# Exchanging softmax statistics between two key sets on VectorE instead of through DRAM

## The chip, the cores and the metric

The kernel runs on one core of a Trainium2 chip. The core has TensorE (PE, matrix products into PSUM), VectorE (DVE), ScalarE (ACT), GpSimd (POOL), and SyncE (SP), which here only issues DMAs. The metric is the device time in microseconds. A separate execution carries the profiler; the trace, the page and every row quoted come from that one. TensorE's clock can be throttled, and the profile lists the granted share of full speed.

## The reference

One block of a hybrid model on 1024 tokens of width 1024, all in fp32. What matters here is the attention part:

```python
q = rms_norm(q.reshape(B, S, N_HEADS, HEAD_DIM), q_norm_g[l]) * HEAD_DIM ** -0.5
k = rms_norm(k.reshape(B, S, N_HEADS, HEAD_DIM), k_norm_g[l])
for window, dilation in ((128, 1), (512, 4), (2048, 16)):
    o_g, lse_g = dilated_window_attention(q, k, v, slopes, window, dilation)
    outs.append(o_g); lses.append(lse_g)
mix = jax.nn.softmax(jnp.stack(lses), axis=0)
o = jnp.einsum('gbsh,gbshd->bshd', mix, jnp.stack(outs))
y_b = o @ w_attn_out[l]
```

There are 16 heads of 64 columns, with a linear distance penalty per head. Each query sees three sets of keys: the last 128 tokens, every fourth token of the last 512, every sixteenth of the last 2048. The three softmaxes, mixed by their log sums, are one softmax in which a key counts as often as it occurs. Beside attention there are a gated convolution branch, gates (a sigmoid of a product of the normed input), an output product and a feed-forward block with a short convolution.

## The kernel before

**Stages.** First come the normed input and a part of the gate and convolution products; then six column groups of queries, keys and values (`qkv_head`, `qkv_tail`, lines 662 to 697), with the 31-tap convolution on VectorE and GpSimd beside them. From about 525 to 900 us of the span stand the sixteen attention heads (lines 776 to 976), then the two output products and the feed-forward block. Every product is made in three matmuls, from a high and a low part of each operand: `split` (line 85) makes the high part on ScalarE and the low one on VectorE.

**Values.** `qkv_head` writes the high and low parts of a group of 128 tokens and eight heads to the DRAM tile `dv`, token by token (line 668). Each token's row of a head is 512 B. `values(h)` (line 779) reads them twice for a head, in six DMAs: `near` holds tokens in the order of 128-token blocks, `same` in the order of the token's residue modulo 4.

**A head.** A head takes eight steps, n = 0 to 7, in the loop at line 931. In each step `score` computes two blocks of 128 queries: a block of 128 consecutive tokens against keys at all distances within its window (`near`), and one residue class against its own class (`same`), whose keys cover the second and third set at once. `tensor_tensor_reduce` on VectorE (line 816) adds the mask, negates and takes the extreme value in one instruction; `powers` on ScalarE (line 823) makes the exponentials and their sums. So the tile `st`, [128, 2, 16, 2], holds in `st[:, 0]` sixteen columns of (negated maximum, sum): eight of the near set, eight of the class set. A query's near numbers and its class numbers stand on different partitions and in different columns.

**The exchange.** To join the two softmaxes of a query, the numbers of one set have to be brought to the places of the other. `exchange_out` (line 828), in step 0 of the next head, stores both halves in DRAM by two SP DMAs. `exchange_in` (line 833), in step 2, reads them back in the other order by two DMAs on ScalarE's queue, into `st[:, 1]`. `factor_first` and `factor_last` (lines 838 to 850) then compute w = exp(min(difference of maxima, 80)) x other sum + own sum; the exponential is on ScalarE, in step MERGE = 4, the rest on GpSimd, and VectorE takes the reciprocal in step 5.

**From there.** `share` (line 855) scales the exponentials by the factor on GpSimd, sixteen operations a head. `flip` (line 861) transposes the scaled blocks on TensorE and splits them into `ph` (ScalarE) and `pl` (VectorE). `weigh` (line 886) multiplies them with the values. BACK = 7 sets how many steps the chain lags: scalings of a head begin in step 5 of the next, transposes in step 7, weighing in the step after that.

**What fills the gaps.** Between these steps TensorE gets products of the gates and of the convolution output, handed out by the generator `gates` (`side_steps`, line 208), three matmuls of 512 columns at a time. `FILL` gives how many such pieces a step takes: 2.7 in the first steps, 1.48 in the body, 2.0 in the tail. Their weights are split in the same stage, high part by a VectorE cast (line 200), low part on GpSimd (line 190). What is left runs in a closing loop (line 974).

**Order.** In the head loop the instructions of ScalarE, VectorE and TensorE run in the order in which they are written (`manual_schedule`). GpSimd and SP are ordered by a planner that simulates the schedule. `head(h)` (line 721) loads q, kh, kl and the mask of a head in seven DMAs. In step 0 they and the six value loads are held behind the second store of the exchange:

```python
if n == 0 and 0 < h <= H:
    with tc.issue_after(exchange_out(h - 1).ins):
        if h + 1 < H:
            tiles[h + 1] = head(h + 1)
        values(h - 1)
```

`order(h, b)` (line 791) rearranges the queries of a head by class on GpSimd, once `q` has been loaded; the rearranged copy feeds the class scores.

Of the kernel before, what the change touches and what calls it, by code (L numbers as in the profile page):

```python
# [13 lines left out]
F32 = mybir.dt.float32  # L14
F32R = mybir.dt.float32r
AF = mybir.ActivationFunctionType
ALU = mybir.AluOpType
# [4 lines left out]
P = 128  # L22
D = 1024
T = 1024
KT = D // P
H = 16
# [7 lines left out]
LAG = 3  # L34
FILL = (2.7, 1.48, 2.0)
MERGE = 4
BACK = 7
SHARE = 0.6
# [22 lines left out]
def block_kernel(ctx: ExitStack, tc: tile.TileContext, x, xT, w_first, g1, g2, pack, mask,  # L61
# [18 lines left out]
    ident = cst.tile([P, P], F32, name="ident")  # L80
# [515 lines left out]
    with tc.tile_pool(name="ph1", bufs=1, reuse_waits="tile") as p1, ExitStack() as rest:  # L596
# [179 lines left out]
    with tc.tile_pool(name="ph2", bufs=1, reuse_waits="tile") as p2:  # L776
        vals, stats, rows, factors = {}, {}, {}, {}

        def values(h):
            near, same = (p2.tile([P, 8, P], F32R, tag=f"v{i}", bufs=2, name=f"v{i}_{h}") for i in range(2))  # L780
            src = dv[h // 8]
            for r in range(4):
                fetch(near[32 * r : 32 * r + 32], src.rearrange("(i j r) h e -> r j i h e", i=8, r=4)[r][:, :, h % 8, :])
            for b in range(2):
                fetch(same[:, 4 * b : 4 * b + 4, :],
                      src.rearrange("(b p r) h e -> b p r h e", b=2, r=4)[b][:, :, h % 8, :])
            vals[h] = near, same
# [3 lines left out]
        def order(h, b):  # L791
            classes[h % 2, b] = t = p2.tile([P, 512], F32R, tag=f"q{b}", bufs=2 - b, name=f"q{b}_{h}")
            q = tiles[h][0][:, 512 * b : 512 * b + 512]
            pool.tensor_copy(t.rearrange("d (r j a) -> d r j a", a=4, r=4), q.rearrange("d (a r j) -> d r j a", a=4, r=4))  # L794

# [28 lines left out]

        far = lambda h, i: dstat[i][h].rearrange("(r j) (a f) -> (j a) r f", r=4, a=4)
        turned = lambda st, i: st[:, i, 8:16, :].rearrange("p (r b) s -> p r (b s)", r=4)

        def exchange_out(h):
            st = stats[h]
            sp.dma_start(dstat[0][h], st[:, 0, 0:8, :])  # L830
            return sp.dma_start(far(h, 1), turned(st, 0))

        def exchange_in(h):
            st = stats[h]
            act.dma_start(turned(st, 1), far(h, 0))
            act.dma_start(st[:, 1, 0:8, :], dstat[1][h])

        def factor_first(h):
            st = stats[h]
            w = p2.tile([P, 16], F32, tag="w", bufs=2, name=f"w_{h}")  # L840
            pool.tensor_tensor(out=w, in0=st[:, 0, :, 0], in1=st[:, 1, :, 0], op=ALU.subtract)
            pool.tensor_scalar(w, w, 80.0, 1.0, op0=ALU.min, op1=ALU.mult)
            return w

        def factor_last(h, w):
            st = stats[h]
            act.activation(w, w, AF.Exp)
            pool.tensor_tensor(out=w, in0=w, in1=st[:, 1, :, 1], op=ALU.mult)
            pool.tensor_tensor(out=w, in0=w, in1=st[:, 0, :, 1], op=ALU.add)
            factors[h] = w  # L850
# [10 lines left out]
        def flip(h, n):  # L861
# [4 lines left out]
            for j, t in enumerate(srcs):  # L866
                o = pp[:, j * P : (j + 1) * P]
                pe.transpose(o.rearrange("p (a j) -> p j a", a=4) if j < 2 - x else o, t, ident)  # L868
            w = len(srcs) * P
# [59 lines left out]
        with tc.manual_schedule(engines={ENG.Activation, ENG.DVE, ENG.PE}):  # L929
            pend = []  # L930
            for at in range(8 * H + 8 + BACK + 1):
# [12 lines left out]
                if n == 0 and 0 < h <= H:  # L944
                    with tc.issue_after(exchange_out(h - 1).ins):
                        if h + 1 < H:
                            tiles[h + 1] = head(h + 1)
                        values(h - 1)
                if n == 2 and 0 < h <= H:
                    exchange_in(h - 1)  # L950
                    w_now = factor_first(h - 1)
                if n == MERGE and 0 < h <= H:
                    factor_last(h - 1, w_now)
                if n == MERGE + 1 and 0 < h <= H:
                    dve.reciprocal(factors[h - 1], factors[h - 1])  # L955
                s0 = at - 6 - BACK
# [556 lines left out]
def _mask():  # L1513
# [5 lines left out]
    near = token[:, None] + P - keys[None, :]  # L1519
    turn = 32 * (at % 4) + at // 4  # L1520
    same = 4 * (turn[:, None] + P - np.arange(2 * P)[None, :])
    dist = np.concatenate([near, same], axis=1)
# [50 lines left out]
```

## Time and profile before

| what | us |
|---|---|
| median of 3 runs (lowest, highest) | 1738.64 (1736.17, 1743.72) |
| the profiled execution | 1745.46 |
| its span | 1743.7 |
| DVE, ACT, POOL busy | 1251.9, 838.9, 532.7 |
| mean granted TensorE clock | 0.992 |

In a row of instructions there stand the line of the kernel, the engine, the operation, the tiles as out<-in, the shape, and behind the bar the busy time in us, the mean duration of one in ns, and the idle time just before. In the timeline a row starts with the start and the duration in us and ends, in brackets, with the engine's idle time before the instruction and what ended it. A row of waits gives the total in us, how often, and the longest. A row of windows gives the stretch and its length, then each engine's busy time (PE, weight loads, DVE, ACT, POOL) with instruction counts, the granted clock, the busy share of the DMA engines, and GB/s. Rows of DMA issues end with the median us from issue to landing.

### The profile page before, as it was taken

To read this page: it belongs to the slowest core of one execution; us is meant where nothing else is said; L and a number is where in the kernel's file an instruction comes from. 1 tells how busy PE (TensorE), PEld (TensorE's weight loads), DVE (VectorE), ACT (ScalarE), POOL (GpSimd) and SP (SyncE) were. 2 spreads that over 40 slices of the span, in tenths; PEclk is the share of its full clock that TensorE was granted. 3 is DMA by queue.
4 is the path that set the end of the run, shared out by engine and by line. 5 is a ranking of instruction groups with operands and counts; after the bars stand their busy time and mean duration, and the time that the engine had idled before them with its cause. 6 is when DMAs were issued, how large, how long until landed. Compare 5 with 4: busy or idle time off the path is not lost.

```text
span 1743.7 us, 23765 instructions
## 1 busy us (share of the span) xinstructions
PE 1705.7 (98%) x8384; PEld 1430.0 (82%) x8384; DVE 1251.9 (72%) x1846; ACT 838.9 (48%) x1482; POOL 532.7 (31%) x575
## 2 busy tenths in 40 slices
PE   9999999999999899988999999999999999999999
PEld 7888888887887788877888888888888888888877
DVE  6999999989843555654645564787767777889863
ACT  5533345454344567655645342555445445533431
POOL 0068739999412566774630000000000000000000
PEclk9999999999999999999999999999999999999999
DMA  8323264553468787898647686622222222499851
GB/s 319 121 97 108 75 235 133 157 175 113 126 241 216 165 187 185 220 225 189 148 121 262 197 308 211 223 97 85 85 85 74 96 84 74 148 337 329 286 167 48
DMA packets 189591, 294.36 MB, mean 169 GB/s; under 512 B 35104, under 2 KB 100896, under 8 KB 189216
## 3 DMA queue, kind: packets, MB, share of 16 engines
q1 hardware_dynamic: 176992, 289.43, 52.5%
q10 hardware_dynamic: 12480, 3.41, 0.9%
q8 instruction: 66, 1.08, 0.3%
q14 instruction: 53, 0.43, 0.1%
HBM read 212.84 MB, written 79.95 MB: 168 GB/s over the span
## 4 chain that ended last, share of the span: by engine, by line
PE 86%; DMA 8%; ACT 2%; POOL 2%; DVE 1%; issue 1%; SPq 0%; ACTq 0%; POOLq 0%; DVEq 0%
PE qkv L151 15%; PE dx L1398 6%; PE xz L131 6%; PE xz L132 6%; PE xz L133 6%; PE wo L151 5%; PE dy L1398 4%; DMA st<-dst 4%; PE glugv L355 3%; PE o L883 3%; PE y L132 2%; PE y L133 2%; PE y L131 2%; PE uxz L133 2%; PE uxz L132 2%; PE uxz L131 2%
## 5 line engine op out<-in xcount | busy, mean ns | idle before, releaser
L636 DVE SCALAR_TENSOR_TENSOR work<-apad,pk,work 128x1024 f32<-128x1024 f32 x188 | 241.6, 1285 | 3.4
L88 DVE TENSOR_TENSOR pl<-pp,ph 128x512 fp32r<-128x512 f32 (+2 forms) x128 | 72.2, 603 | 91.7 <-ACT ph L87 91.5
L823 ACT ACTIVATE p<-p,st 128x256 f32<-128x256 f32 (+1 forms) x256 | 119.2, 469 | 19.9 <-DVE st L816 15.0
L816 DVE CUSTOM_DVE_ANT_0 p<-s,m 128x256 f32<-128x256 f32 (+1 forms) x256 | 86.8, 377 | 52.6 <-PE s L810 49.7
L151 PE MATMUL qkv<-hi_qkv,hT 128*128 128x512 f32 x384 | 115.0, 393 | 0.0
L859 POOL TENSOR_SCALAR p<-p,w 128x256 f32<-128x256 f32 (+1 forms) x256 | 111.5, 459 | 6.1 <-DVE w L955 5.6
L1301 DVE SCALAR_TENSOR_TENSOR u<-u,pk 128x1023 f32<-128x1023 f32 x88 | 112.3, 1278 | 1.0 <-ACT u L1299 0.7
L627 POOL TENSOR_TENSOR part<-prod,part 128x1024 f32<-128x1024 f32 x43 | 103.5, 2407 | 21.3 <-ACT prod L626 16.7
L87 ACT ACTIVATE ph<-pp 128x512 fp32r<-128x512 f32 (+2 forms) x128 | 61.4, 529 | 80.4 <-PE pp L868 76.3
L883 PE MATMUL o<-ph,v 128*128 128x128 f32 (+1 forms) x336 | 74.3, 279 | 20.6 <-ACT ph L87 20.6
L883 PEld LDWEIGHTS o<-ph,v 128*128 128x128 f32 x336 | 63.6, 194 | 29.9 <-ACT ph L87 24.9
L151 PEld LDWEIGHTS qkv<-hi_qkv,hT 128*128 128x128 f32 x384 | 71.4, 188 | 14.6
L88 DVE TENSOR_TENSOR lo_uv<-raw_uv,hi_uv 128x1024 fp32r<-128x1024 f32 x20 | 24.5, 1226 | 79.6 <-ACT hi_uv L87 79.6
L883 PE MATMUL o<-pl,v 128*64 128x128 f32 (+1 forms) x336 | 77.6, 248 | 3.2 <-DVE pl L88 3.2
L151 PE MATMUL wo<-hi_wo,mT 128*128 128x512 f32 x256 | 80.1, 391 | 0.0
L112 POOL TENSOR_TENSOR s<-s,mhalf 128x1 f32<-128x1 f32 x8 | 5.3, 662 | 214.9 <-issue 174.1
L794 POOL CAST q<-q 128x512 fp32r<-128x512 f32 x32 | 35.9, 1123 | 109.6 <-DMA q<-dq 88.8
L131 PE MATMUL xz<-blk_t,hi_s3g 128*128 128x512 f32 x176 | 68.6, 390 | 0.7 <-ACT xc L1275 0.7
L131 PE MATMUL xz<-h2left,hi_uv 128*128 128x512 f32 x176 | 68.6, 390 | 0.0
L133 PE MATMUL xz<-h2left,lo_uv 128*128 128x512 f32 x176 | 68.5, 389 | 0.0
L132 PE MATMUL xz<-blk_t,hi_s3g 128*128 128x512 f32 x176 | 68.5, 389 | 0.0
L132 PE MATMUL xz<-h2left,hi_uv 128*128 128x512 f32 x176 | 68.5, 389 | 0.0
(398 smaller groups left out, 5356.9 us busy)
## 6 DMA issues: line engine op xcount, KB each, us to landing
wr<-w_down SPq DMA_DIRECT2D x45, 512.0 KB, 5.5
gr<-dff SPq DMA_DIRECT2D x62, 256.0 KB, 5.0
raw_qkv<-w_qkv SPq DMA_DIRECT2D x24, 512.0 KB, 4.4
dff<-u SPq DMA_DIRECT2D x22, 512.0 KB, 2.6
raw_uv<-w_up SPq DMA_DIRECT2D x21, 512.0 KB, 3.2
raw_ug<-w_up SPq DMA_DIRECT2D x20, 512.0 KB, 3.2
q<-dq SPq DMA_DIRECT2D x32, 256.0 KB, 5.3
dv<-v SPq DMA_DIRECT2D x16, 512.0 KB, 2.7
```

The source lines that it names most:

```text
L88: by.tensor_tensor(out=lo, in0=src, in1=hi.bitcast(F32), op=ALU.subtract)
L131: pe.matmul(o, wh[:, k, :], bh[:, k, :], start=(start and k == 0), stop=False, skip_group_check=not start)
L132: pe.matmul(o, wh[:, k, :], bl[:, k, :], start=False, stop=False, skip_group_check=not start)
L133: end = pe.matmul(o, wl[:, k, :], bh[:, k, :], start=False, stop=(k == 3), skip_group_check=not start)
L151: pe.matmul(ps, l, r[:, k % 2, :], start=(n == 1), stop=(n == 3 * KT))
L627: pool.tensor_tensor(out=a[:, CW - 1 :] if j == CW - 1 else part, in0=prods[j % 3], in1=part, op=ALU.add)
L636: dve.scalar_tensor_tensor(out=a[:, CW - 1 :] if j == CW - 1 else work, in0=a[:, j : j + T], scalar=w(c, j), in1=part if j == n else work, ...
L823: act.activation(pt, pt, AF.Exp, bias=st[:, 0, at, 0:1], scale=-1.0, accum_out=st[:, 0, at, 1:2])
L859: pool.tensor_scalar(pt, pt, f, 1.0, op0=ALU.mult, op1=ALU.mult)
L883: pe.matmul(view(o[:m]), v[:, :m], t, start=(start and i == 0), stop=(stop and i == 0), skip_group_check=True)
L1301: dve.scalar_tensor_tensor(out=acc[:, d:], in0=src[:, : T - d], scalar=w(2 - d), in1=acc[:, d:], op0=ALU.mult, op1=ALU.add)
L1398: pe.matmul(banks[n], a[:, c], b[:, d], start=(start and i == 0 and m == 0), stop=(stop and i == nf - 1 and m == 2), skip_group_check=True)
```

## The change

The numbers of the two sets are no longer sent through DRAM. Class blocks keep their queries in the order (block, position) instead of (position, block), so that what is exchanged are whole blocks of 32 partitions. `exchange` moves them with eight VectorE copies: one of the tile, two of 64 partitions, one more of the tile, four of 32 partitions. VectorE also takes the subtraction, the clamp, the products and the sum of the factor that GpSimd did; sums and maxima of the other set are read with their two halves of columns swapped. The exchange and the value loads stand in step 1, the exponential in step 2 (MERGE), the factor in step 3; BACK is 6; FILL's middle rate is 1.52.

Values are stored twice, once in each order in which they are read: in `dv`, a partition's eight blocks of a head lie in a row of 4 KB, and in `dt`, a head's tokens lie one after the other, so that four make 2 KB. A group of 128 tokens is written by two DMAs in pieces of 512 B. The transposes and the mask follow the new order.

```diff
-FILL = (2.7, 1.48, 2.0)
-MERGE = 4
-BACK = 7
+FILL = (2.7, 1.52, 2.0)
+MERGE = 2
+BACK = 6
...
-    dv = [dr.tile([T, 8, P], F32R, name=f"dv{i}") for i in range(2)]
-    dstat = [[dr.tile([P, 16], F32, name=f"dst{i}_{h}") for h in range(H)] for i in range(2)]
+    dv = [dr.tile([P, 8, 8, P], F32R, name=f"dv{i}") for i in range(2)]
+    dt = [dr.tile([8, T, P], F32R, name=f"dt{i}") for i in range(2)]
...
-                spill(dv[g8][tt * P : (tt + 1) * P], vt.rearrange("p h s d -> p h (s d)"))
+                flat = vt.rearrange("p h s d -> p h (s d)")
+                spill(dv[g8][:, :, tt, :], flat)
+                spill(dt[g8][:, tt * P : (tt + 1) * P, :].rearrange("h p e -> p h e"), flat)
...
-            src = dv[h // 8]
+            src = dv[h // 8].rearrange("(j r) h i e -> r j h i e", r=4)
             for r in range(4):
-                fetch(near[32 * r : 32 * r + 32], src.rearrange("(i j r) h e -> r j i h e", i=8, r=4)[r][:, :, h % 8, :])
+                fetch(near[32 * r : 32 * r + 32], src[r][:, h % 8])
+            src = dt[h // 8][h % 8].rearrange("(b p r) e -> b p (r e)", b=2, r=4)
             for b in range(2):
-                fetch(same[:, 4 * b : 4 * b + 4, :],
-                      src.rearrange("(b p r) h e -> b p r h e", b=2, r=4)[b][:, :, h % 8, :])
+                fetch(same[:, 4 * b : 4 * b + 4, :].rearrange("p r e -> p (r e)"), src[b])
...
-            pool.tensor_copy(t.rearrange("d (r j a) -> d r j a", a=4, r=4), q.rearrange("d (a r j) -> d r j a", a=4, r=4))
+            pool.tensor_copy(t.rearrange("d (r a j) -> d r a j", a=4, r=4), q.rearrange("d (a r j) -> d r a j", a=4, r=4))
...
+        def exchange(h):
             st = stats[h]
+            half = p2.tile([P, 2, 2, 8], F32, tag="sh", bufs=2, name=f"sh_{h}")
+            own = st[:, 0].rearrange("p (g u v) s -> p g u (v s)", g=2, u=2)
+            dve.tensor_copy(half, own)
+            for u in range(2):
+                dve.tensor_copy(half[u * 64 : u * 64 + 64, :, 1 - u], own[64 - u * 64 : 128 - u * 64, :, u])
+            far = st[:, 1].rearrange("p (w v b) s -> p w v (b s)", w=4, v=2)
+            mid = half.rearrange("p g u (v f) -> p (g u) v f", v=2)
+            dve.tensor_copy(far, mid)
+            for v in range(2):
+                for c in (0, 64):
+                    dve.tensor_copy(far[c + 32 * v : c + 32 * v + 32, :, 1 - v], mid[c + 32 - 32 * v : c + 64 - 32 * v, :, v])
+            w = p2.tile([P, 16], F32, tag="w", bufs=2, name=f"w_{h}")
+            for g in range(2):
+                dve.tensor_tensor(out=w[:, 8 * g : 8 * g + 8], in0=st[:, 0, 8 * g : 8 * g + 8, 0],
+                                   in1=st[:, 1, 8 - 8 * g : 16 - 8 * g, 0], op=ALU.subtract)
+            dve.tensor_scalar(w, w, 80.0, 1.0, op0=ALU.min, op1=ALU.mult)
+            return w
+
+        def factor(h, w):
             st = stats[h]
+            for g in range(2):
+                dve.tensor_tensor(out=w[:, 8 * g : 8 * g + 8], in0=w[:, 8 * g : 8 * g + 8],
+                                   in1=st[:, 1, 8 - 8 * g : 16 - 8 * g, 1], op=ALU.mult)
+            dve.tensor_tensor(out=w, in0=w, in1=st[:, 0, :, 1], op=ALU.add)
+            dve.reciprocal(w, w)
             factors[h] = w
...
-                o = pp[:, j * P : (j + 1) * P]
-                pe.transpose(o.rearrange("p (a j) -> p j a", a=4) if j < 2 - x else o, t, ident)
+                pe.transpose(pp[:, j * P : (j + 1) * P], t, ident)
...
                 if n == 0 and 0 < h <= H:
-                    with tc.issue_after(exchange_out(h - 1).ins):
-                        if h + 1 < H:
-                            tiles[h + 1] = head(h + 1)
-                        values(h - 1)
-                if n == 2 and 0 < h <= H:
-                    exchange_in(h - 1)
-                    w_now = factor_first(h - 1)
+                    if h + 1 < H:
+                        tiles[h + 1] = head(h + 1)
+                if n == 1 and 0 < h <= H:
+                    values(h - 1)
+                    w_now = exchange(h - 1)
                 if n == MERGE and 0 < h <= H:
-                    factor_last(h - 1, w_now)
+                    act.activation(w_now, w_now, AF.Exp)
                 if n == MERGE + 1 and 0 < h <= H:
-                    dve.reciprocal(factors[h - 1], factors[h - 1])
+                    factor(h - 1, w_now)
```

More of the change, by code (lines that the diff above doesn't have):

```diff
@@ L823, in powers @@
             act.activation(pt, pt, AF.Exp, bias=st[:, 0, at, 0:1], scale=-1.0, accum_out=st[:, 0, at, 1:2])
-        far = lambda h, i: dstat[i][h].rearrange("(r j) (a f) -> (j a) r f", r=4, a=4)
-        turned = lambda st, i: st[:, i, 8:16, :].rearrange("p (r b) s -> p r (b s)", r=4)
-        def exchange_out(h):
+        def exchange(h):
             st = stats[h]
-            sp.dma_start(dstat[0][h], st[:, 0, 0:8, :])
-            return sp.dma_start(far(h, 1), turned(st, 0))
-        def exchange_in(h):
-            st = stats[h]
-            act.dma_start(turned(st, 1), far(h, 0))
-            act.dma_start(st[:, 1, 0:8, :], dstat[1][h])
@@ L838, in factor_first @@
[L838 to L849, printed above, removed]
+            half = p2.tile([P, 2, 2, 8], F32, tag="sh", bufs=2, name=f"sh_{h}")
@@ L1519, in _mask @@
     near = token[:, None] + P - keys[None, :]
-    turn = 32 * (at % 4) + at // 4
-    same = 4 * (turn[:, None] + P - np.arange(2 * P)[None, :])
+    same = 4 * (at[:, None] + P - np.arange(2 * P)[None, :])
     dist = np.concatenate([near, same], axis=1)
```

## The prediction

> **What bounds the kernel now.** I read the page first (busy shares, then the chain that ended last), then TensorE's time by windows, its waits, its granted clock behind each long wait, and last the timeline of one head with a gap and one without.
>
> ```profile
> span 1743.7 us, 23765 instructions
> ...
> PE   1705.7 (98%) x8384; PEld 1430.0 (82%) x8384; DVE 1251.9 (72%) x1846; ACT 838.9 (48%) x1482; POOL 532.7 (31%) x575
> ```
> TensorE is the bound; only 38.0 us of the span are idle on it. The windows say where:
>
> ```profile
> 525.00:900.00 375.00, 349.22 (x2294) 307.85 (x2294) 200.18 (x728) 224.96 (x715) 215.87 (x394) 0.97 0.77 184
> ```
> 25.8 us of them, 375.00 - 349.22, lie in the sixteen attention heads, at a granted clock of 0.97. TensorE's waits there:
>
> ```profile
> PE o L883 <- ACT ph L87: 20.6, 11, 4.3
> PE o L883 <- DVE pl L88: 3.2, 12, 0.3
> PE pp L868 <- POOL p L859: 1.8, 1, 1.8
> ```
> Nearly all of it is one kind: the weighing matmul waits for `ph`, which ScalarE has not made. The timeline of the longest gap shows why:
>
> ```profile
> 808.56 0.33 SPq L830 DMA_DIRECT2D dst<-st  x1
> ...
> 812.21 0.39 ACTq L835 DMA_DIRECT2D st<-dst  x1
> ...
> 824.26 0.23 POOL L841 TENSOR_TENSOR w<-st 128x16 f32<-128x16 f32 x1 [7.19 <-DMA st<-dst]
> ...
> 824.90 0.21 ACT L847 ACTIVATE w<-w 128x16 f32<-128x16 f32 x1 [5.80 <-POOL w L842]
> ...
> 826.66 0.33 PE L883 MATMUL o<-ph,v 128*128 128x128 f32 x1 [4.28 <-ACT ph L87]
> ```
> The statistics leave at 808.6 and return only by 824.3. Meanwhile ScalarE stands 5.8 us at the small exponential, in order, with the next `ph` queued behind it. A head in which the exchange returns in time, beside that one:
>
> ```profile
> 616.18:634.61 18.43, 18.43 (x133) 16.58 (x133) 11.56 (x45) 13.46 (x45) 10.32 (x22) 1.00 0.91 212
> ...
> 808.56:834.44 25.88, 21.34 (x143) 19.21 (x142) 11.30 (x44) 13.55 (x45) 11.08 (x24) 0.93 0.62 135
> ```
> Without the gap a head is TensorE end to end (18.43 of 18.43) at full clock. The other head lost 4.5 us of TensorE and ran at 0.93.
>
> **The price of the waits removed.** Idle time is 25.8. The clock is the second part: windows behind the long gaps, and one behind a shorter gap.
>
> ```profile
> 564.00:572.00 8.00, 7.87 (x30) 6.16 (x31) 1.86 (x7) 3.20 (x11) 7.08 (x15) 0.57 0.43 112
> 608.00:616.00 8.00, 7.34 (x40) 6.50 (x41) 4.20 (x14) 5.50 (x16) 7.91 (x18) 0.79 0.20 78
> 650.00:658.00 8.00, 7.26 (x48) 6.07 (x49) 5.73 (x21) 7.00 (x22) 7.91 (x18) 1.00 0.67 218
> 755.00:763.00 8.00, 7.35 (x41) 6.61 (x42) 4.93 (x15) 5.34 (x17) 7.69 (x17) 0.79 0.76 279
> 777.00:785.00 8.00, 6.92 (x38) 6.25 (x39) 5.46 (x17) 5.85 (x19) 7.75 (x17) 0.79 0.81 260
> 801.00:809.00 8.00, 6.94 (x38) 6.24 (x39) 4.84 (x17) 5.83 (x18) 7.61 (x19) 0.79 0.67 205
> 826.00:834.00 8.00, 7.07 (x39) 6.27 (x40) 3.64 (x13) 4.80 (x16) 7.87 (x17) 0.79 0.30 103
> ```
> Lost clock: 8 x 0.43 = 3.4 in the first and 8 x 0.21 = 1.68 in each of five, 11.8 in all; none at 650. The pool is 25.8 + 11.8 = 37.6 us, 2.35 a head. Two of the gaps behind which the clock fell were short:
>
> ```profile
> 777.81 0.33 PE L883 MATMUL o<-ph,v 128*128 128x128 f32 x1 [1.25 <-ACT ph L87]
> ...
> 801.80 0.33 PE L883 MATMUL o<-ph,v 128*128 128x128 f32 x1 [2.71 <-ACT ph L87]
> ```
> The Trainium skill, "TensorE: Matmul & The Clock Gate", Part 1 (What's actually happening), halves the clock after an idle window of about 3.4 us and restores it after as long a busy one. Its price, half of 3.4, agrees with the 1.68; its condition doesn't hold for these two gaps, nor for the 1.8 us wait for GpSimd ahead of the window at 564. By its letter the three return no clock, 3.4 + 2 x 1.68 = 6.8 us less, and the sum below would come to 1718; I go by the rows.
>
> **What the change adds on VectorE.** Per head: eight copies, two subtractions and a clamp at step 1, then two products and a sum at step 3; the reciprocal stays. No row shows a copy of 32 partitions. The nearest, a tiny two-input operation and an operation that crosses 64 partitions for odd heads:
>
> ```profile
> L1109 DVE TENSOR_TENSOR s<-ss 128x1 f32<-128x1 f32 x8 | 1.3, 160 | 6.2 <-ACT wo L1105 6.2
> ...
> L912 DVE TENSOR_TENSOR op<-o,ot 64x512 f32<-64x512 f32 x32 | 21.8, 682 | 3.4 <-ACT ot L911 2.9
> ```
> L912 costs 682 ns whether it crosses or not (its 32 cases hold both), so crossing looks free and I take 0.16 us for each: 11 x 0.16 = 1.76 at step 1, 3 x 0.16 = 0.48 at step 3. Behind the block on VectorE stand step 2's score maxima and the `pl` pair of step 2, for which the next weighing matmul waits. The cover is VectorE's idle time between two `pl` pairs, in the undisturbed head:
>
> ```profile
> 617.40 0.42 DVE L816 CUSTOM_DVE_ANT_0 p<-s,m 128x256 f32<-128x256 f32 x1 [0.40 <-PE s L810]
> 619.74 1.29 DVE L88 TENSOR_TENSOR pl<-pp,ph 128x512 fp32r<-128x512 f32 x2 [1.70 <-ACT ph L87]
> 622.47 0.43 DVE L816 CUSTOM_DVE_ANT_0 p<-s,m 128x256 f32<-128x256 f32 x1 [0.89 <-PE s L810]
> 623.98 0.56 DVE L88 TENSOR_TENSOR pl<-pp,ph 128x384 fp32r<-128x384 f32 x1 [0.87 <-ACT ph L87]
> ```
> 0.40 + 1.70 = 2.10 in one pair of steps, 0.89 + 0.87 = 1.76 in the next. So 1.76 fits, with nothing to spare. What is pushed onto TensorE lies between 0 and 2.24 a head (no cover at all); I take 0.5, 8.0 in all, nearer to nothing because the idle time is there; a push so short costs no clock by the 650 row. The block itself waits for step 7's sums of the head before, a full step old. ScalarE's exponential (step 2) then waits for VectorE, with `ph` behind it, but a transpose of step 2 has to come between.
>
> **What moves at no cost.** Gone are four DMAs a head: two on SP, after which seven loads of head(h+1) no longer stand, and two on ScalarE's queue; GpSimd loses four operations of `w`. The six value loads go behind the seven head loads, at step 1; their first use moves to step 7, six steps or some 14 us later. Their pieces grow from 512 B to 2 and 4 KB; I count the relief at nothing. With one step less of BACK the factors are due at step 3 for transposes from step 6 (before: 5 and 7), and the tail loses a step, which gate products (two a step) fill now; 0. FILL shifts gate products from the closing loop into the heads: the same matmuls. The contiguous transposes, query order and mask keep their counts; 0.
>
> The value spills double, 16 to 32 issues and 512 B pieces:
>
> ```profile
> dv<-v SPq DMA_DIRECT2D x16, 512.0 KB, 2.7
> ...
> dq<-qh SPq DMA_DIRECT2D x16, 256.0 KB, 2.5
> ...
> 510.00:520.00 10.00, 10.00 (x46) 8.29 (x45) 8.81 (x11) 9.62 (x13) 2.22 (x2) 1.00 1.01 406
> ```
> The `dq` spills write 256 KB in 512 B pieces and land in 2.5 us, so the piece size alone isn't dear, and TensorE is busy (10.00 of 10.00) over it. But at 510 the DMA engines are full. Three late extra spills of 2.7 us could hold back the gate weights by up to 8 us; I take 2 (0 to 8).
>
> **Sum**, against the profiled execution's own 1745.46 us: -25.8 - 11.8 + 8.0 + 2.0 = -27.6, 1717.9. The median shown is 0.9961 of that execution, so 1711.
>
> **The rivals.**
>
> *All of it goes*: no push, no spill cost: 1745.46 - 37.6, scaled 1701. For it: undisturbed heads have no idle TensorE at all. Against: VectorE has nothing to spare.
>
> *VectorE and GpSimd get in each other's way.* VectorE's single-input casts in this stage:
>
> ```profile
> L200 DVE CAST hi_co<-raw_co 128x512 fp32r<-128x512 f32 x16 | 11.9, 744 | 0.0
> ...
> L200 DVE CAST aT<-raw_a 128x512 fp32r<-128x512 f32 x16 | 8.2, 510 | 0.0
> ...
> L200 DVE CAST hi_gt<-raw_gt 128x512 fp32r<-128x512 f32 x12 | 6.1, 506 | 0.0
> ...
> L200 DVE CAST hi_gt<-raw_gt x12: 417/422/978, 538.8 to 651.2; 128x512 fp32r<-128x512 f32 x12
> ...
> 844.10 1.47 POOL L190 TENSOR_TENSOR lo_co<-raw_co,hi_co 128x512 fp32r<-128x512 f32 x1
> 844.54 1.30 DVE L200 CAST hi_co<-raw_co 128x512 fp32r<-128x512 f32 x1
> ```
> (11.9 + 8.2 + 6.1) / 44 = 0.60 us on average, where the median of `hi_gt` (the middle of the three values in its row, in ns) is 0.42. So a cast pays 0.18 on average, and 0.88 in the pair shown, where it ends just after GpSimd's operation. With 0.18 on each of the eleven the block is 3.74, 1.8 over the mean idle time of 1.93: 16 x 1.8 = 28.8 in place of 8.0 gives 1732. Against: GpSimd works for 10.32 of 18.43 us, and mostly later in the head. The Trainium skill, "SBUF — State Buffer", section Who interferes with whom, speaks against this change: a VectorE copy in a two-port mode, or one with two SBUF inputs against a reading GpSimd operation, blocks fully until the other ends. The pair above agrees.
>
> *The query load takes the exchange's place.* The cast of the next head's queries stands ahead of the scalings on GpSimd:
>
> ```profile
> 834.44 0.32 SPq L830 DMA_DIRECT2D dst<-st  x1
> ...
> 843.00 1.14 POOL L794 CAST q<-q 128x512 fp32r<-128x512 f32 x1 [9.03 <-DMA q<-dq]
> ...
> L859 POOL TENSOR_SCALAR p<-p,w 128x256 f32<-128x256 f32 (+1 forms) x256 | 111.5, 459 | 6.1 <-DVE w L955 5.6
> ```
> It ended 9.7 us into this head. Step 6 begins about 6/8 x 18.43 = 13.8 in, and seven scalings of 0.46 must precede: 10.6. Were it 3 us later, 2 us a head would be lost, 32 in place of 8.0: 1735, no change that can be told. For it: DMA is 0.91 busy in fast heads. Against: fewer, larger pieces.
>
> *Slower: the block falls among the scalings.* If each of the eleven waits for one scaling, 11 x (0.16 + 0.46) = 6.8, 4.9 over the idle time, and 1.68 of clock: 6.6 x 16 = 105 against 37.6, so 1745.46 + 105 + 2 - 37.6, scaled 1808. It decides once a head loses over 2.35, a block over 4.3 us, 0.39 an operation. Against: scalings start with step 3's factors and last 16 x 0.46 = 7.4 us, so end before the next step 1.
>
> **How the numbers follow.** Forecast 0.60, all goes 0.14, ports 0.13, query load 0.08, slower 0.05. A change under 0.5% (8.7 us) can't be told from none. Faster: 0.60 + 0.14 + half of the ports case = 0.80; the same: the other half and the query load, 0.15; slower 0.05. The range runs from 1699 (all goes, and a little from the loads) to 1732 (the ports case), leaving out the last two.
>
> **What would show it.** Right: no wait of TensorE for `ph` over 0.8 us between 525 and 880, granted clock 1.00 there, heads of 18.5 to 19.5 us, copies near 0.16 us each, ScalarE's small exponential without its 5 us waits. Wrong: copies of 0.4 us or more, `pl` late behind them on VectorE, or GpSimd's casts waiting longer for `q`; a gap near 520 would be the spills.

## The result, and the profile after

| | before | after |
|---|---|---|
| median of 4 runs (lowest, highest), us | 1738.3 (1736.17, 1743.72) | 1710.53 (1708.97, 1710.87) |
| the profiled execution, us | 1745.46 | 1710.68 |
| mean granted TensorE clock | 0.992 | 0.999 |

The ratio of the two, taken over all the runs, is 0.9834, with a 95% interval of 0.9811 to 0.9857 (the medians alone give 0.9840): the kernel is faster by 1.7%, and the 1711 us forecast is met. The two profiled executions lie further apart than the medians, by 34.8 us against 27.8. That difference is taken up below.

First the head of the page of the kernel after, to be held against the one shown of before:

```profile
span 1708.9 us, 23809 instructions
...
PE 1691.5 (99%) x8384; PEld 1420.4 (83%) x8384; DVE 1290.2 (75%) x2070; ACT 838.6 (49%) x1482; POOL 501.2 (29%) x511
```

TensorE's idle time in the span fell from 38.0 to 17.4 us (1708.9 - 1691.5), and TensorE's busy time fell by 14.2 us although it has the same 8384 matmuls: that is the clock. VectorE took on 38 us and 224 instructions (14 for each of the 16 heads) and GpSimd gave up 31.5 us. The windows, the first the one quoted of before, the second 15 heads from one exchange to the same point 15 heads later:

```profile
525.00:900.00 375.00, 367.72 (x2448) 325.52 (x2447) 254.72 (x970) 244.92 (x741) 185.44 (x330) 1.00 0.75 211
548.19:843.05 294.86, 290.98 (x2040) 261.22 (x2039) 220.20 (x885) 205.71 (x659) 172.35 (x308) 1.00 0.78 214
```

In the first row 25.8 us of idle TensorE have become 7.3, at a granted clock of 1.00 in place of 0.97. (More of the stretch now lies behind the heads, which end earlier; the waits below that lie in the heads add up to 5.1.) A head takes 294.86 / 15 = 19.66 us. TensorE's waits, then ScalarE's, in the same stretch:

```profile
PE o L887 <- ACT ph L87: 1.6, 4, 0.5
PE o L887 <- DVE pl L88: 1.5, 5, 0.4
PE yb L123 <- ACT hi_ao L87: 1.5, 1, 1.5
PE pp L872 <- POOL p L864: 1.3, 1, 1.3
PE s L809 <- DMA kl<-dk: 0.7, 1, 0.7
```
```profile
ACT w L955 <- DVE w L845: 24.3, 15, 4.1
```

The 20.6 us for `ph` are 1.6, none over 0.5. ScalarE still stands at the small exponential (L955), 24.3 us over the heads, but this wait is now hidden nearly everywhere: the `ph` behind it isn't due yet. A wait is worth only what is late behind it. The timeline of an undisturbed exchange on VectorE:

```profile
648.03 0.18 DVE L832 COPY sh<-st 128x32 f32<-128x32 f32 x1
648.24 0.35 DVE L834 COPY sh<-st 64x16 f32<-64x16 f32 x2
648.63 0.18 DVE L837 COPY st<-sh 128x32 f32<-128x32 f32 x1
648.84 0.71 DVE L840 COPY st<-sh 32x16 f32<-32x16 f32 x4
649.58 0.24 DVE L843 TENSOR_TENSOR w<-st 128x8 f32<-128x8 f32 x2
649.86 0.18 DVE L845 TENSOR_SCALAR w<-w 128x16 f32<-128x16 f32 x1
...
651.21 1.02 DVE L88 TENSOR_TENSOR pl<-pp,ph 128x384 fp32r<-128x384 f32 x2 [0.59 <-ACT ph L87]
```

The block takes 2.0 us (648.03 to 650.04), and VectorE then still waits 0.59 us for ScalarE before its `pl` pair: the block fits. In nine of the sixteen heads the block is longer than 2.1 us, and in all nine an operation of GpSimd runs beside it; in five the first copy is stretched, in four a later operation. Here is the head with the longest first copy, one of the two that cost TensorE most, with GpSimd's row:

```profile
746.62 1.28 POOL L191 TENSOR_TENSOR aT<-raw_a,aT 128x512 fp32r<-128x512 f32 x1
...
746.66 1.28 DVE L832 COPY sh<-st 128x32 f32<-128x32 f32 x1
...
749.80 0.22 ACT L955 ACTIVATE w<-w 128x16 f32<-128x16 f32 x1 [2.26 <-DVE w L845]
...
750.45 0.33 PE L887 MATMUL o<-ph,v 128*128 128x128 f32 x1 [0.34 <-ACT ph L87]
...
751.18 0.27 PE L887 MATMUL o<-pl,v 128*64 128x128 f32 x1 [0.40 <-DVE pl L88]
```

A copy of 0.18 us takes 1.28 here, exactly as long as the GpSimd subtraction that began 0.04 us ahead of it; the exchange is late by that much, and TensorE loses 0.74 us (0.79 in the other one, behind the block at 628.7). Over all sixteen heads the block has a mean length of 2.45 us, from the first copy's start to the clamp's end in the timeline (2.00 to 3.64).

### The profile page after: what moved, and what is told of

The parts are those of the page before. It is cut to its first block, busy times and chain, and to the rows that moved or that the text cites. A ratio compares the mean times of both kernels' runs of the same rounds, so it can differ in the third digit from the quotient of the medians.

```text
span 1708.9 us, 23809 instructions
## 1 busy us (share of the span) xinstructions
PE 1691.5 (99%) x8384; PEld 1420.4 (83%) x8384; DVE 1290.2 (75%) x2070; ACT 838.6 (49%) x1482; POOL 501.2 (29%) x511
## 4 chain that ended last, share of the span: by engine, by line
PE 90%; DMA 4%; DVE 3%; ACT 1%; issue 1%; SPq 0%; POOL 0%; ACTq 0%; DVEq 0%
PE qkv L151 14%; PE dx L1400 7%; PE xz L131 6%; PE xz L133 6%; PE xz L132 6%; PE dy L1400 5%; PE wo L151 5%; PE o L887 3%; PE glugv L356 3%; PE pp L872 2%; PE y L133 2%; PE y L132 2%; PE y L131 2%; PE uxz L132 2%; PE uxz L131 2%; PE uxz L133 2%
## 5 line engine op out<-in xcount | busy, mean ns | idle before, releaser
L132 PE MATMUL xz<-blk_t,hi_s3g 128*128 128x512 f32 x176 | 68.5, 389 | 0.0
L133 PE MATMUL xz<-h2left,lo_uv 128*128 128x512 f32 x176 | 68.5, 389 | 0.0
L132 PE MATMUL xz<-h2left,hi_uv 128*128 128x512 f32 x176 | 68.5, 389 | 0.0
L133 PE MATMUL xz<-blk_t,lo_s3g 128*128 128x512 f32 x176 | 68.5, 389 | 0.0
```

Source lines behind the costliest of these rows:

```text
L132: pe.matmul(o, wh[:, k, :], bl[:, k, :], start=False, stop=False, skip_group_check=not start)
L133: end = pe.matmul(o, wl[:, k, :], bh[:, k, :], start=False, stop=(k == 3), skip_group_check=not start)
```

## The experiments

My theory: the gain is the exchange's trip through DRAM alone; the two layouts, the order of issue and the constants carry nothing; the new block costs what the prediction's sum said, about 0.5 us a head, since it just fits between two pairs of `pl` evictions. The rivals are named at each run. Ratios are against the kernel before in the same set of runs, with 95% intervals; its medians in the three sets were 1738.7, 1741.9 and 1740.2.

### The exchange alone, with the values laid out as before

```diff
-    dv = [dr.tile([P, 8, 8, P], F32R, name=f"dv{i}") for i in range(2)]
-    dt = [dr.tile([8, T, P], F32R, name=f"dt{i}") for i in range(2)]
+    dv = [dr.tile([T, 8, P], F32R, name=f"dv{i}") for i in range(2)]
...
-                spill(dt[g8][:, tt * P : (tt + 1) * P, :].rearrange("h p e -> p h e"), flat)
```

> The changed kernel with the values stored and read as before (one copy in DRAM, reads in 512 B pieces). Theory (TensorE's waits for the exchange's return were nearly all of the gain): 1710 to 1716, no wait of TensorE for ph over 0.8 us, granted clock in the heads 0.99 or 1.00. Rival (the larger value pieces relieve the DMA engines, and that is the gain): 1725 or more, gaps and clock losses stay.

It took 1707.86 us (1706.21 to 1710.85), ratio 0.9818 (0.9785 to 0.985), a little under the range expected. The second layout isn't needed for the gain. It may cost a little: in this run's trace the two waits for `kl` and for GpSimd's `p` (0.7 and 1.3 us in the kernel after) are missing. The intervals of the two kernels overlap, so the 2.7 us between their medians are a sign and no proof. With that reserve it is the fastest full version of all the kernels run here, ahead of before and after.

### The value layouts alone, on the kernel before

```diff
-    dv = [dr.tile([T, 8, P], F32R, name=f"dv{i}") for i in range(2)]
+    dv = [dr.tile([P, 8, 8, P], F32R, name=f"dv{i}") for i in range(2)]
+    dt = [dr.tile([8, T, P], F32R, name=f"dt{i}") for i in range(2)]
...
-            src = dv[h // 8]
+            src = dv[h // 8].rearrange("(j r) h i e -> r j h i e", r=4)
```

> The kernel before with only the two value layouts (spills and reads) of the changed one; the numbers still go through DRAM. Theory: the exchange's reads still queue with 1.75 MB of head loads, so long waits for ph remain: 1726 to 1740, granted clock in the heads below 0.99. Rival (DMA relief is the gain): 1708 to 1718.

1740.33 us, ratio 1.0007 (0.9985 to 1.0029): nothing, and at the upper edge of what was expected. TensorE's wait for `ph` is still there:

```profile
PE o L886 <- ACT ph L87: 18.3, 11, 4.6
```

### The kernel after with the old constants

```diff
-FILL = (2.7, 1.52, 2.0)
-MERGE = 2
-BACK = 6
+FILL = (2.7, 1.48, 2.0)
+MERGE = 4
+BACK = 7
```

> The changed kernel with FILL's middle rate 1.48, MERGE 4 and BACK 7. Theory: the constants carry nothing by themselves: 1709 to 1715. Rival (the shorter lag and the fill rate make a part of the gain): 1718 or more.

1735.26 us, ratio 0.9973 (0.9951 to 0.9994). Here my theory fell: with the old constants the exchange on VectorE gives next to nothing. The long wait is a new one, for `pl`:

```profile
PE o L887 <- DVE pl L88: 20.9, 15, 5.0
```

The timeline of its longest case shows how it comes about:

```profile
734.85 1.47 POOL L191 TENSOR_TENSOR aT<-raw_a,aT 128x512 fp32r<-128x512 f32 x1
...
735.64 0.72 DVE L832 COPY sh<-st 128x32 f32<-128x32 f32 x1
...
736.40 1.73 DVE L834 COPY sh<-st 64x16 f32<-64x16 f32 x2
...
736.83 1.26 POOL L191 TENSOR_TENSOR aT<-raw_a,aT 128x512 fp32r<-128x512 f32 x1
...
738.05 1.26 POOL L191 TENSOR_TENSOR lo_co<-raw_co,hi_co 128x512 fp32r<-128x512 f32 x1
...
738.16 1.19 DVE L837 COPY st<-sh 128x32 f32<-128x32 f32 x1
...
740.49 1.28 DVE L88 TENSOR_TENSOR pl<-pp,ph 128x512 fp32r<-128x512 f32 x2
...
741.23 0.37 PE L887 MATMUL o<-pl,v 128*64 128x128 f32 x1 [5.01 <-DVE pl L88]
```

The `pl` pair stands directly behind the block on VectorE. Transposes come in every second step. With BACK = 7 they fall in odd steps, where the exchange (step 1) and the factor also are; with BACK = 6 in even ones, so that the scores of the next step stand between the block and the next pair. The place alone isn't the cause, though. The block shown takes 4.93 us and not 2.0: three of its operations end just as an operation of GpSimd ends. In four of the sixteen heads the block keeps its 2.0 us, and no such wait follows there; in the twelve others it takes 2.2 to 4.9 us (mean of all 3.26), GpSimd works beside it each time, and each is followed by such a wait. In the kernel after, blocks of up to 3.64 us cost TensorE at most 0.8 us. So it takes both, a stretched block and a pair directly behind it. Which of the three constants does it is the next question.

### The eight copies made twice

```diff
             for v in range(2):
                 for c in (0, 64):
                     dve.tensor_copy(far[c + 32 * v : c + 32 * v + 32, :, 1 - v], mid[c + 32 - 32 * v : c + 64 - 32 * v, :, v])
+            dve.tensor_copy(half, own)
+            for u in range(2):
+                dve.tensor_copy(half[u * 64 : u * 64 + 64, :, 1 - u], own[64 - u * 64 : 128 - u * 64, :, u])
+            dve.tensor_copy(far, mid)
+            for v in range(2):
+                for c in (0, 64):
+                    dve.tensor_copy(far[c + 32 * v : c + 32 * v + 32, :, 1 - v], mid[c + 32 - 32 * v : c + 64 - 32 * v, :, v])
```

> The changed kernel with the eight copies of the exchange made twice in a row, some 1.35 us more on VectorE in step 1 of each head. Theory (the block just fits VectorE's idle time between two pl pairs, 0.6 us left in the head at 650): 0.7 us a head pushed onto TensorE, 12 in all: 1718 to 1726. Rival (VectorE has ample cover): 1709 to 1713. Rival (ports: each further copy also waits for GpSimd): 1730 or more, with gaps over 1.5 us.

1728.87 us, ratio 0.9938 (0.9913 to 0.9963): 18 us more than the kernel after, between the two expectations. The block's mean length grew from 2.45 to 4.08 us, by 1.63, and a head by 18.3 / 16 = 1.1: about seven tenths of what is added reaches TensorE. Its place is the one the prediction named, ScalarE's exponential waiting for VectorE, with `ph` behind it:

```profile
PE o L894 <- ACT ph L87: 10.8, 9, 2.1
```

### BACK alone put back to 7

```diff
-BACK = 6
+BACK = 7
```

> The kernel after with one constant put back: BACK 7 in place of 6, MERGE 2 and FILL 1.52 kept. Theory (parity): with a lag of 7 the transposes and their two evictions fall in the odd steps, so the exchange block (about 2 us of VectorE, step 1) and the factors (0.7 us, step 3) are queued directly ahead of a step's pl evictions, as they were in the run with all three old constants; then 1728 to 1738 us, PE's waits for pl and ph together over 12 us between 525 and 880. Rival (the lag is free, MERGE 4 or the fill constant made the loss): 1708 to 1714 us and waits as in the kernel after, about 3 us.

1723.45 us, ratio 0.991 (0.9881 to 0.9938). It is 13 us slower than the kernel after, by this one number, with waits of 9.8 us for `pl` and 1.6 for `ph`. The direction is the parity theory's and its rival is out, but time and waits both stay under what it expected; the size is half of what the three constants cost together. Seven of the `pl` waits (9.4 us) follow the seven blocks that take 2.96 us or more; behind the nine of 2.0 to 2.3 us none does. The other 12 us belong to MERGE (4 puts the factor in step 5, so nearer to the scalings) or FILL; that wasn't separated. The mean block is 2.79 us here and 3.26 with all three old constants, so GpSimd's operations fall into it more often there.

### A lag of 7 with the exchange in even steps

```diff
-MERGE = 2
-BACK = 6
+MERGE = 3
+BACK = 7
...
                 if n == 1 and 0 < h <= H:
                     values(h - 1)
+                if n == 2 and 0 < h <= H:
                     w_now = exchange(h - 1)
```

> The kernel after with BACK 7 and everything of the exchange one step later: the block at step 2, the exponential at step 3, the factors at step 4; the value loads stay at step 1. The transposes are then in odd steps and the block in even ones, as apart as in the kernel after. Theory (parity, not the lag, is what counts): 1707 to 1716 us, PE's waits for pl and ph under 6 us. Rival (a longer lag costs by itself, through buffers held longer): as with BACK 7 alone, 1725 to 1738 us.

1715.54 us, ratio 0.9859 (0.9827 to 0.9892), waits 3.1 us for `pl` and 2.5 for `ph`. Moving the block to the other kind of step gave back 8 of the 13 us. Most of what BACK did here is thus the place of the block among the steps: against the pairs behind it, and against GpSimd's operations (the mean block is back at 2.46 us). Some 4 to 5 us remain, for the longer lag or the later place of the exchange; their cause stays open.

### The copies left out

```diff
-            half = p2.tile([P, 2, 2, 8], F32, tag="sh", bufs=2, name=f"sh_{h}")
...
-                                   in1=st[:, 1, 8 - 8 * g : 16 - 8 * g, 0], op=ALU.subtract)
+                                   in1=st[:, 0, 8 - 8 * g : 16 - 8 * g, 0], op=ALU.subtract)
```

> The kernel after without the eight block copies per head: the differences and products are taken from the partition's own maxima and sums, so the output is not the reference's; all else stays. It prices the copies. Theory (the block fits between two pairs of evictions and pushes little): 1705 to 1710 us, at most 5 us under the kernel after, PE's remaining waits for ph and pl down from about 3 us to about 1. Rival (the copies still cost some 0.5 us in each head, as the prediction took): 1698 to 1704 us.

1703.41 us, ratio 0.9792 (0.9764 to 0.9819). That is the rival's range and not my theory's. The copies cost 7.1 us by the medians (those of the two kernels are from different sets, but no run of the one reaches the other's), 0.44 a head, where the prediction took 0.5 for the whole block; in the stretch of the heads TensorE then idles 2.65 us, and the 1.3 and 0.6 us for GpSimd's `p` and for `kl` are what is left there:

```profile
525.00:900.00 375.00, 372.35 (x2480) 331.40 (x2479) 239.90 (x850) 248.23 (x746) 186.29 (x330) 1.00 0.76 216
```

Taking the copies' 2.0 us away (the mean block of 2.45 less 0.46 for its last three instructions) gave 0.44 a head; adding 1.63 cost 1.1. So the cover ends about where the block does, as the prediction said.

### The kernel before without any exchange

```diff
                 if n == 0 and 0 < h <= H:
-                    with tc.issue_after(exchange_out(h - 1).ins):
-                        if h + 1 < H:
-                            tiles[h + 1] = head(h + 1)
-                        values(h - 1)
+                    if h + 1 < H:
+                        tiles[h + 1] = head(h + 1)
+                    values(h - 1)
                 if n == 2 and 0 < h <= H:
-                    exchange_in(h - 1)
...
-            pool.tensor_tensor(out=w, in0=st[:, 0, :, 0], in1=st[:, 1, :, 0], op=ALU.subtract)
+            pool.tensor_tensor(out=w, in0=st[:, 0, :, 0], in1=st[:, 0, :, 0], op=ALU.subtract)
```

> The kernel before with the exchange through DRAM left out: no transfers of maxima and sums, the factors are computed by the same instructions from the partition's own numbers, so the output is not the reference's; constants, layouts and the place of the head and value loads are those of before. Theory (the 25 us of idle TensorE and the lost clock hang on the exchange's landing alone): 1700 to 1714 us, no wait of TensorE for ph over 1 us between 525 and 880. Rival (the head and value loads, or the instructions on GpSimd, hold the heads as well): 1722 to 1738 us.

1710.04 us, ratio 0.9827 (0.9799 to 0.9855). With the old constants, layouts and order of loads, and GpSimd's four operations still there, the trip through DRAM accounts for 31.9 us. The rivals for the cause of the old waits are out: no wait for `ph` stands in the list for 525 to 900 any more, which reads:

```profile
PE o L870 <- DVE pl L88: 3.2, 4, 1.7
PE s L806 <- DVE st L816: 1.7, 1, 1.7
```

### The loads behind the exchange's reads

```diff
                 if n == 0 and 0 < h <= H:
-                    with tc.issue_after(exchange_out(h - 1).ins):
+                    exchange_out(h - 1)
+                if n == 2 and 0 < h <= H:
+                    with tc.issue_after(exchange_in(h - 1).ins):
                         if h + 1 < H:
                             tiles[h + 1] = head(h + 1)
                         values(h - 1)
-                if n == 2 and 0 < h <= H:
-                    exchange_in(h - 1)
```

> The kernel before with one order changed: the next head's loads and the value loads are issued behind the exchange's two reads (in step 2) and not between its writes and its reads. Everything else is that of before. Theory (the exchange's four small transfers are late because 1.75 to 2.75 MB of loads stand in the DMA engines ahead of the reads): TensorE's waits for ph and pl between 525 and 880 fall from 24 us to under 10, and the time lies at 1710 to 1725 us, near the kernel without any exchange (1710). Rival (two trips to DRAM and back are too long by themselves): no change, 1733 to 1745 us, the waits still some 20 us.

1724.7 us (1719.98 to 1728.3), ratio 0.9915 (0.9893 to 0.9936). The order of the queue is about half of the matter: in the profiled execution, the shortest of these, the waits for `ph` and `pl` in the heads are down to 4.3 and 3.2 us. The times to landing in the heads, first of before, then of this run:

```profile
dst<-st SPq DMA_DIRECT2D x32, 8.0 KB, 2.6
st<-dst ACTq DMA_DIRECT2D x32, 8.0 KB, 7.9
```
```profile
dst<-st SPq DMA_DIRECT2D x32, 8.0 KB, 5.7
st<-dst ACTq DMA_DIRECT2D x32, 8.0 KB, 3.8
```

The reads land in half the time, the stores in twice. From the first store's issue to GpSimd's subtraction the timeline gives 13.0 us before (mean of 14 heads, up to 15.8) and 10.7 here (15 heads, up to 12.4). Whether the rest is still the loads, now those of the head before, or the way to DRAM and back itself, wasn't separated.

### The constants alone, on the kernel before

```diff
-FILL = (2.7, 1.48, 2.0)
-MERGE = 4
-BACK = 7
+FILL = (2.7, 1.52, 2.0)
+MERGE = 3
+BACK = 6
```

> The kernel before with the new constants alone: BACK 6, FILL 1.52, and MERGE 3 (the merge can't come at step 2 there, where the reads are only issued). Theory (the shorter lag only pays once the exchange no longer goes through DRAM; here it takes one step, about 2.4 us, from the exchange's slack): no gain or a loss, 1738 to 1760 us, waits for ph and pl 20 us or more. Rival (the constants are the gain, and the copies ride along): 1710 to 1725 us.

1793.38 us, ratio 1.031 (1.0282 to 1.0337): 53 us slower, more than I expected. A step less of lag is a step less for a trip of 13 us, and nearly every head now waits (13 times):

```profile
PE o L883 <- ACT ph L87: 50.5, 13, 7.2
```

### The kernel after once more

No edit; it stands in one set with the two runs before it and the next.

> The kernel after once more, on the same chip and beside the same runs of before as the others of this call: 1708 to 1712 us if the time is a matter of the kernel alone, and a ratio within 0.002 of the first one, 0.983.

1711.79 us (1709.58 to 1715.8), ratio 0.9845 (0.9822 to 0.9868): the first result again.

### The block cut in two

```diff
                     values(h - 1)
-                    w_now = exchange(h - 1)
-                if n == MERGE and 0 < h <= H:
-                    act.activation(w_now, w_now, AF.Exp)
+                    half_now = exchange(h - 1)
...
                 piece_high(2)
+                if n == 1 and 0 < h <= H:
+                    w_now = exchange_last(h - 1, half_now)
+                if n == MERGE and 0 < h <= H:
+                    act.activation(w_now, w_now, AF.Exp)
```

Here `exchange` ends after the first three copies, and `exchange_last` holds the rest of it. The value layout, not shown, is the one of the first experiment.

> The kernel after with the old value layout (1707.9 us by itself) and the exchange block cut in two: the first three copies stay at the beginning of step 1, the other five with the subtraction and clamp go to the step's end, behind its scores; the small exponential goes to the end of step 2. Theory (what the block still costs, 7 us of copies, is the scores and evictions that it pushes at one place): two halves of about 0.9 and 1.1 us push less, 1701 to 1706 us. Rival (the copies cost their time wherever they stand, since VectorE's work comes at its own rate): 1706 to 1711 us.

1713.67 us, ratio 0.9856 (0.9834 to 0.9878): 5.8 us slower than the same kernel with the block in one piece, and outside both expectations. The scores of the step already stood ahead of the block on VectorE, so that the cut let nothing through but a cast of a weight (L200), and the cast sets GpSimd going:

```profile
746.81 1.28 POOL L190 TENSOR_TENSOR aT<-raw_a,aT 128x512 fp32r<-128x512 f32 x1
746.85 1.28 DVE L829 COPY sh<-st 128x32 f32<-128x32 f32 x1
...
748.55 0.43 DVE L200 CAST aT<-raw_a 128x512 fp32r<-128x512 f32 x1
...
749.06 1.29 POOL L190 TENSOR_TENSOR aT<-raw_a,aT 128x512 fp32r<-128x512 f32 x1 [0.97 <-DVE aT L200]
749.10 1.81 DVE L841 COPY st<-sh 32x16 f32<-32x16 f32 x4
...
752.51 0.27 PE L888 MATMUL o<-pl,v 128*64 128x128 f32 x1 [2.10 <-DVE pl L88]
```

GpSimd's second subtraction waits for that cast and then falls into the second half: here two copies are held by 1.1 us each instead of one. In the uncut kernel, the cast comes behind the block. The mean length, from first copy to clamp, is 3.23 us against 2.62 for the same kernel uncut. That the exponential stands later as well rides along and wasn't separated.

## Why the prediction was right, point by point

**The pool.** The sum's first terms, 25.8 us of idle TensorE and 11.8 of lost clock, were read from one profiled execution. The direct test of their 37.6 is the kernel before without any exchange, and it is 31.9 us faster, 5.7 less. The prediction counted all idle time of TensorE; of its waits, 3.2 us for `pl` and 1.8 for GpSimd had nothing to do with the trip, and without the trip 4.9 us of waits still stand there. The kernel without copies, which has neither the trip nor the new block's copies, is 38.5 us under before by the medians of the same set. The 6.6 us between these two come from other parts of the change (constants, layouts, query order, the factor on VectorE), which the prediction put at 0 or at a cost; they weren't separated. Between the profiles, idle time in the heads went from 25.8 to about 5 us, and the clock from 0.97 to 1.00.

**The push.** 8.0 us were forecast for the block; 7.1 were measured by leaving its eight copies out, and its last three operations have no price of their own. The reason given, a cover of 1.76 to 2.10 us for a block of 1.76, holds: less block gives little, more block costs about seven tenths of its length. The block is somewhat longer than 11 x 0.16. Undisturbed it takes 2.0 us, and the mean is 2.45; the difference is GpSimd's.

**The spills.** 2.0 us were taken, for gate weights held back near 520 us. No such wait is there: the list of TensorE's waits for 500 to 530 is empty. The two waits that are missing without the second layout add up to 2.0 us, but they stand at 544 and 562, and a wait for GpSimd's `p` (1.8 us) is in the kernel before too. The median without the layout is 2.7 lower, with overlapping intervals. The size may be right; the reason given isn't shown.

**The step that failed: "What moves at no cost".** There I priced the constants at 0, "the tail loses a step, which gate products (two a step) fill now; 0". As a price of the new constants that is harmless. As a statement of what carries the gain it is wrong: without them the copies bring 3 us and not 28, and alone they cost 53. The gain needs both, or the old lag with the block a step later (1715.5 us). The short lag became possible when the trip vanished, and it moves the `pl` pairs out of the steps in which the block stands. I had computed the cover from a head of before without asking in which step, relative to the transposes and to GpSimd's operations, the block would stand under each constant; the forecast came out because the change had the matching pair.

**The loads and the queries**, in the same paragraph. The value loads do not all go behind the seven head loads: in the trace of after, five of them are issued at 658.9 and 659.3 and the next head's `q` at 661.2. It costs nothing that a wait shows. And the contiguous query order wasn't nothing for GpSimd, whose cast takes about half as long (the rows stand below).

**The scaling.** The sum gave -27.6 against the profiled execution, and the profiles differ by -34.8; the factor 0.9961 then took another 6.8 off, and the median was met. So two things met in the total. The profiled run of before was the longest of those shown, 6.8 above its median; that of after lies on its median. In the 29 runs of before in one set the time goes with the granted clock, from 1728.2 us at 0.996 to 1750.3 at 0.991, so a pool read from a long run is probably larger than a typical one. And the costs were too large as well: the whole change brings 27.8 us and leaving the trip out 31.9, so what came in place of the trip costs 4.1 us net (the medians of these two kernels, from different sets, lie only 0.5 apart), where the sum had 10.0. Two errors of about 6 us with opposite signs cancel. That the total came out within 1 us is luck; that the trip held the heads, and that the block's copies cost about half a us a head, is not.

**The rivals.** *All of it goes* (1701) is near what the copies' absence gives, 1703.4; the copies are what holds it off. *VectorE and GpSimd in each other's way* is real, and small in the kernel after: not each operation pays 0.18 us, but in five heads the first copy alone pays 0.23 to 1.1 us, and the mean block is 0.45 longer than an undisturbed one, where the rival had 1.98. With the old constants it is 1.26 longer, and the waits for `pl` follow it. So the rival's mechanism, with the place of the block, undoes the gain there. The Trainium skill, "SBUF — State Buffer", section Who interferes with whom, has a VectorE copy in a two-port mode wait until a GpSimd operation that started first ends; the pair at 746.6 agrees to a few hundredths of a us, and the cut block shows it a second time. In which mode these copies run, no run here shows. The argument against that rival, that GpSimd works mostly later in the head, was too weak: its scalings do, but weight subtractions also fall into step 1. *The query load* did not come: GpSimd's waits for `q` fell from 88.8 to 68.5 us, and TensorE waits for GpSimd once, 1.3 us. *Slower* did not come, and doubling the copies (a mean block of 4.08 us, under the 4.3 that the prediction gave as its point) stayed faster than before, which fits.

**The signs.** Waits for `ph` (at most 0.5 us, under 0.8), the clock, and copies near 0.16 us in the median came as said. Heads of 19.66 us are just over the 18.5 to 19.5 given. ScalarE's 5 us waits were to vanish; 24.3 us of them stayed, the longest 4.1, hidden.

## What to carry to other kernels

Before pricing a block on an in-order engine, write down in which step of the pipeline it stands and in which the evictions behind it stand: here moving the same block from one kind of step to the other was worth 8 us of 13. A small transfer that must return before a deadline isn't priced by its size alone but also by what is queued ahead of it: here putting those loads behind it recovered half. Of a change with several parts, run each part alone before naming the one that pays: here the layouts gave nothing, the copies with the old constants 0.3% and the constants a loss of 3%, and only copies with constants that suit their place won. When one engine's short operations can be held by another's long ones, look up what the other engine does at that place too: here nearly all the waits for `pl` followed blocks that were held.

## What the runs showed of the hardware that I had not expected

A copy of 32 partitions and 16 columns that crosses partitions costs nearly as much as one of the whole tile in place; the prediction had taken 0.16 us for each without a row of such a copy. The first line of each answer gives the shortest, the middle and the longest in ns:

```profile
L840 DVE COPY st<-sh x64: 161/166/173, 549.0 to 845.4; 32x16 f32<-32x16 f32 x64
```
```profile
L832 DVE COPY sh<-st x16: 175/177/1279, 548.2 to 843.0; 128x32 f32<-128x32 f32 x16
```

GpSimd's cast of 128x512 elements depends on the order in which it reads and writes. Before, then after, where runs of queries stay contiguous, at the same size:

```profile
L794 POOL CAST q<-q 128x512 fp32r<-128x512 f32 x32 | 35.9, 1123 | 109.6 <-DMA q<-dq 88.8 <-issue 20.8
```
```profile
L797 POOL CAST q<-q 128x512 fp32r<-128x512 f32 x32 | 20.0, 628 | 89.5 <-DMA q<-dq 68.5 <-DVE apad L720 20.8 <-PE s L813 0.2
```

Behind a gap the clock falls or not at nearly the same length. In the cut-block kernel a gap of 2.06 us ended at 730.74 and one of 2.10 at 752.51; the windows behind them:

```profile
730.00:734.00 4.00, 3.26 (x23) 2.99 (x24) 3.93 (x16) 2.62 (x10) 1.29 (x1) 1.00 1.00 390
752.00:756.00 4.00, 3.49 (x13) 3.00 (x14) 3.79 (x16) 1.89 (x9) 0.87 (x3) 0.66 1.02 360
```

The clock is the column behind GpSimd's: 1.00 and 0.66. The Trainium skill, "TensorE: Matmul & The Clock Gate", Part 1 (What's actually happening), names an idle window of about 3.4 us as the condition; this gap of 2.10 us was enough, one of 2.06 wasn't, and what decides between them no run here shows. Had the prediction gone by the letter, it would have said 1718.
